# Attention output projection in a decoder trunk: two partial sums moved into the residual, twelve products beside each step, and one norm's squares summed on VectorE

## The chip, the cores and the metric

The kernel runs on one core of one Trainium2 chip. A core has a matrix engine (TensorE, PE in the profile; its weight loads are PEld), VectorE (DVE), ScalarE (ACT), GpSimd (POOL) and SyncE (SP), which here issues the loads from memory. Each engine works through its own instructions in a fixed order and waits on semaphores where it needs another engine's result. Matrix products are accumulated in PSUM, of which the kernel uses all eight banks, each 128 partitions by 512 floats. The metric is the device time of one execution in microseconds (us), lower is better. Differences of about 0.2% (2.3 us) are as much as such a measurement can tell from no change.

## The reference

A trunk of two layers over 512 positions of width 1024. Layer 0 mixes tokens with a gated MLP, then a gated feed-forward part with a causal convolution, then a gated embedding. Layer 1 uses sliding-window attention with 16 query heads over 4 shared key/value heads; its output projection is added to the residual, and the same kind of feed-forward part follows. The part that matters here:

```python
def rmsnorm(x, g):
    xf = x.astype(jnp.float32)
    y = xf * lax.rsqrt(jnp.mean(xf * xf, axis=-1, keepdims=True) + EPS)
    return (y * g.astype(jnp.float32)).astype(x.dtype)

def mixer_b(xn, w_q, sinks, w_o, kblk, vblk):        # layer 1
    ...
    probs = e / (jnp.sum(e, axis=-1, keepdims=True) + jnp.exp(sink - m))
    out = jnp.einsum('bnkgij,bnjkd->bnikgd', probs.astype(vblk.dtype), vblk)
    return out.reshape(B, S, N_Q_HEADS * HEAD_DIM) @ w_o

# in the layer loop
h = h + mixer_b(xn, b_w_q[b], b_sinks[b], b_w_o[b], kblk, vblk)
h = h + conv_ffn(rmsnorm(h, norm_ffn[i]), f_w_up[i], f_conv_w[i], f_conv_b[i], f_w_down[i])
```

## The kernel before

**Layout.** Activations lie feature-major: the residual is eight tiles `h[0]` to `h[7]`, each 128 features by 512 positions. Every matrix product is done in a split form to keep float32 accuracy: both operands are cut into a high and a low part, and `mm3` (lines 184 to 192) issues three matmuls of 128x128 by 128x512 for each block of 128 rows of the contraction: high by high, high by low, low by high. In this text a *product* is one such matmul; a whole row block of 1024 features needs 8 x 3 = 24 products.

**Weights.** Weight pieces come from memory on SP's queue (`load`, line 136) into raw buffers, and each unit of 1024 columns is cut by ScalarE (`wh`, line 163) and VectorE (`wl`, line 164). There are four `wh` and four `wl` buffers. A piece of the output projection is 2048 columns, that is two units: unit one serves contraction blocks 0 to 3, unit two serves blocks 4 to 7, for two row blocks `m`. `chunk` asks for a piece, and `more` (line 741) asks for one unit ahead of its use.

**The attention stage.** Sixteen steps `i`, one for each of 4 head groups `g` and 4 blocks of 128 positions `n`, with `n` fastest. `scores(i)` makes the score products (`sc`, lines 793, 794), masks and takes minima on VectorE (lines 796, 800) and exponentials on ScalarE (805); `weights(i)` normalizes (813, 815); `turn(i)` transposes on the matrix engine (`tr`, 830) and cuts the result (`pts`, `p`, lines 261, 262; for `n` > 0 GpSimd masks a second copy, 838); `mix(i)` multiplies with the values (`pv`, 852; four products, two where `n` is 0) and `finish(i)` leaves two 128x128 pieces of the attention output in `o2[2g]` and `o2[2g+1]` (872, 875). So `o2[0:2]` belongs to group 0, `o2[2:4]` to group 1, `o2[4:6]` to group 2 (steps 8 to 11), `o2[6:8]` to group 3 (steps 12 to 15). The loop:

```python
for i in range(last + 2):            # last = 16, LATE = 14
    if i < last:
        with tc.high_priority():
            scores(i)
    if LATE <= i < last + 1:
        finish(i - 3)
    if i <= last:
        fill(i)
    if i >= 2:
        mix(i - 2)
    ...
        with tc.high_priority():
            turn(i - 1)
```

**Work beside the steps.** `fill(i)` issues what the table `beside` (line 745) lists for step `i`: other products that keep the matrix engine fed while a step's softmax runs on the other engines. Steps 0 to 9 carry the query projections of later groups, twelve products or more each. Steps 10 to 17 carry parts of the output projection: `merge(m, k0, k1)` (line 732) adds contraction blocks `k0` to `k1` of row block `m` into its PSUM bank `o{m}`, which it holds from its first block to its last. In the table of before, steps 10 to 12 have 12 products, step 13 has 9, step 14 has 15, step 15 has 12, and steps 16 and 17 have 18 each.

**After the steps** (lines 906 to 911) each row block gets its missing products, VectorE adds the bank to `h[m]` (line 910), and `nf.take(m)` (line 295) prepares the next norm: ScalarE scales and rounds (`nf10h`, 257), VectorE makes the low part (`nf10l`, 258), ScalarE squares (`nf1sq`, 287), and GpSimd adds the squares up (`nf1acc`, line 292), all but the last block's, which VectorE adds. The feed-forward part starts on `nf10h`, `nf10l`. Its first up-projection `up(0)` has two halves of 24 products; between them, in the matrix engine's order, stand the products of `norm.begin()` (`nf1ms`, 312), which need the complete sum of squares turned and reduced on VectorE (`nf1turn` 302, `nf1quarter` 304).

**Order.** A scheduler orders each engine's instructions ahead of time, by the program's order as priority, and takes a later instruction first where an earlier one is not ready by its own estimate. PSUM banks and weight buffers are given from a pool of free ones. Lines 190 to 192, 163, 164, 257, 258, 261, 262, 287 and 292 are helpers shared by all stages, so a row is told apart by its tile names.

Of the kernel before, what the change touches and what calls it, by code (L numbers as in the profile page):

```python
# [13 lines left out]
P = 128  # L14
D = 1024
S = 512
KD = D // P
# [31 lines left out]
def tile_yoco(ctx: ExitStack, tc: tile.TileContext, t, out: bass.AP, out_b: bass.AP):  # L49
    nc = tc.nc  # L50
# [10 lines left out]
    def psum(name):  # L61
        return mmp.tile([P, S], F32, tag="mm", name=name)
# [111 lines left out]
    def chunk(cols, kk, ahead=WBUFS):  # L174

        pump(state["next"] + ahead)
        parts = []
        while len(parts) < kk:
            wh, wl, n = take()
            parts += [(wh, wl, j * cols) for j in range(n // cols)]  # L180
        assert len(parts) == kk
        return parts

    def mm3(ps, parts, xs, c0, n=P, first=True, last=True):

        for k, ((wh, wl, off), (xh, xl)) in enumerate(zip(parts, xs)):
            a, b = off + c0, off + c0 + n
            st = first and k == 0
            en = last and k == len(parts) - 1
            nc.tensor.matmul(ps, wh[:, a:b], xh, start=st, stop=False)  # L190
            nc.tensor.matmul(ps, wh[:, a:b], xl, start=False, stop=False)  # L191
            nc.tensor.matmul(ps, wl[:, a:b], xh, start=False, stop=en)  # L192
# [19 lines left out]
    h = [hp.tile([P, S], F32, tag=f"h{k}", name=f"h{k}") for k in range(KD)]  # L212
# [141 lines left out]
    def gain(name, l=0):  # L354
        return lambda k: v(name, l * KD + k)
# [215 lines left out]
    for c in range(4):  # L571
# [4 lines left out]
        for j in range(2):  # L576
            m = 2 * c + j
# [18 lines left out]
    nf = Norm("nf0", [(xp, "x", gain("norm_ffn", 0))])  # L596
# [106 lines left out]
    box = {}  # L703
# [25 lines left out]
        if k1 == KD:  # L729
            qs[g] += queries(box["qp"], g, j)  # L730

    def merge(m, k0, k1):

        if m // 2 not in box:
            box[m // 2] = chunk(256, KD, ahead=2)
        if k0 == 0:
            box[f"o{m}"] = psum(f"o{m}")
        mm3(box[f"o{m}"], box[m // 2][k0:k1], o2[k0:k1], m % 2 * P, first=k0 == 0, last=k1 == KD)
        box[f"k{m}"] = k1

    def more():

# [12 lines left out]
        8: [(project, 3, 1, 0, 4)],  # L755
        9: [(project, 3, 1, 4, 8)],
        10: [(merge, 0, 0, 2), (merge, 1, 0, 2), (more,)],
        11: [(merge, 2, 0, 2), (merge, 3, 0, 2), (more,)],
        12: [(merge, 0, 2, 4), (merge, 1, 2, 4), (more,)],
        13: [(merge, 2, 2, 4), (merge, 3, 2, 3)],  # L760
        14: [(merge, 3, 3, 4), (merge, 0, 4, 6), (merge, 1, 4, 6)],
        15: [(merge, 2, 4, 6), (merge, 3, 4, 6)],
        16: [(merge, 4, 0, 6)],
        17: [(merge, 5, 0, 6)],
    }

    def fill(i):
# [3 lines left out]
    o2 = [[ap.tile([P, S], F32R, tag=f"a{x}{m}", name=f"o{x}{m}") for x in "hl"] for m in range(KD)]  # L771
# [105 lines left out]
    last = len(steps)  # L877
# [28 lines left out]
    nf = Norm("nf1", [(xp, "x", gain("norm_ffn", 1))])  # L906
    for c in range(4):
        for m in (2 * c, 2 * c + 1):
            merge(m, box.get(f"k{m}", 0), KD)
            nc.vector.tensor_add(h[m], h[m], box[f"o{m}"])  # L910
            nf.take(m)

    npl = Norm("np1", [(xp, "x", gain("norm_ple", 1))])
    pef, pet = ffn(1, nf, npl)
# [4 lines left out]
    first = [(a[:, half], b[:, half]) for a, b in xs]  # L919
# [215 lines left out]
```

## Time and profile before

| what | us |
|---|---|
| time, median of 3 runs | 1144.05 |
| lowest and highest of these runs | 1143.8, 1144.77 |
| the profiled execution's own time | 1145.29 |
| its span, first to last instruction | 1143.6 |
| matrix engine busy in the span | 1129.7 |
| VectorE busy | 750.5 |
| ScalarE busy | 521.3 |
| GpSimd busy | 124.5 |
| HBM traffic | 96 GB/s over the span |

The profile is of one execution. Its rows give start and duration in us from the span's start; the number in square brackets behind a row of the timeline is how long the engine stood idle before it, with the instruction that ended the wait. Matmuls are pipelined: a 128x512 product is shown with 0.39 us but follows the one before it after about 0.23 us, so starts are compared and durations of matmuls are not added. In tables by stretch the columns are the length, then busy time and number of instructions of PE, PEld, DVE, ACT and POOL, then the granted clock of the matrix engine (1.00 is full), the share of the DMA engines and their rate.

### The profile page before, as it was taken

The numbers are of one execution on the slowest core, as the hardware profiler recorded it, in microseconds if no ns is written. First come the engines' busy times: TensorE is split into PE (matmuls) and PEld (weight loads), VectorE is DVE, ScalarE is ACT, GpSimd is POOL, SyncE is SP. The second block draws the span as 40 slices with busy tenths as digits, with TensorE's granted clock in tenths as the row PEclk, the third lists the DMA queues.
The fourth block names the chain that finished last, engine by engine and source line by source line (L and its number), as shares of the span: only waits on it lengthen the run. The fifth ranks groups of instructions, "written<-read, shape, count | busy, mean of one in ns | idle before, by whom it ended". The sixth has DMA issues, their size and how long they took to land.

```text
span 1143.6 us, 13592 instructions
## 1 busy us (share of the span) xinstructions
PE 1129.7 (99%) x5266; PEld 942.5 (82%) x5266; DVE 750.5 (66%) x1142; ACT 521.3 (46%) x843; POOL 124.5 (11%) x191
## 2 busy tenths in 40 slices
PE   9999999999999999999999989999999999999997
PEld 7888888888888888888898877788888888888896
DVE  7366477762677367557988967777636763675675
ACT  6534344441343235445656865444313432355562
POOL 2000300000000000021124654000000000000222
PEclk9999999999999999999999999999999999999999
DMA  8322323323223322332224413223232233224302
GB/s 299 144 81 74 111 77 108 110 75 111 93 83 101 111 92 75 129 111 74 74 74 129 129 39 143 83 106 111 74 111 99 76 101 111 92 76 165 111 1 74
DMA packets 25775, 115.40 MB, mean 101 GB/s; under 512 B 2920, under 2 KB 8176, under 8 KB 16240
## 3 DMA queue, kind: packets, MB, share of 16 engines
q1 hardware_dynamic: 25152, 113.89, 29.4%
q8 instruction: 41, 0.67, 0.2%
q10 hardware_dynamic: 560, 0.66, 0.2%
q14 instruction: 22, 0.18, 0.1%
HBM read 108.24 MB, written 2.11 MB: 96 GB/s over the span
## 4 chain that ended last, share of the span: by engine, by line
PE 93%; DVE 4%; issue 1%; ACT 1%; DMA 0%; POOL 0%; SPq 0%; POOLq 0%; DVEq 0%
PE up L190 14%; PE up L191 14%; PE up L192 14%; PE d L190 8%; PE d L192 8%; PE d L191 8%; PE gate L190 2%; PE gate L191 2%; PE gate L192 2%; PE q L190 1%; PE q L192 1%; PE q L191 1%; PE u L191 1%; PE u L192 1%; PE u L190 1%
## 5 line engine op out<-in xcount | busy, mean ns | idle before, releaser
L163 ACT CAST wh<-wraw 128x1024 fp32r<-128x1024 f32 (+2 forms) x197 | 201.8, 1028 | 264.7 <-PE d L191 123.9
L164 DVE TENSOR_TENSOR wl<-wraw,wh 128x1024 fp32r<-128x1024 f32 (+1 forms) x198 | 239.2, 1209 | 126.4 <-ACT wh L163 126.1
L191 PE MATMUL up<-nf10l,wh 128*128 128x512 f32 x352 | 137.8, 391 | 0.4 <-DVE nf10l L258 0.4
L190 PE MATMUL up<-nf10h,wh 128*128 128x512 f32 x352 | 137.7, 391 | 0.0
L192 PE MATMUL up<-nf10h,wl 128*128 128x512 f32 x352 | 137.5, 391 | 0.0
L190 PE MATMUL up<-nf00h,wh 128*128 128x512 f32 x352 | 137.1, 390 | 0.0
L191 PE MATMUL up<-nf00l,wh 128*128 128x512 f32 x352 | 136.9, 389 | 0.0
L192 PE MATMUL up<-nf00h,wl 128*128 128x512 f32 x352 | 136.9, 389 | 0.0
L190 PE MATMUL d<-ah,wh 128*128 128x512 f32 x352 | 136.9, 389 | 0.0
L191 PE MATMUL d<-al,wh 128*128 128x512 f32 x352 | 136.9, 389 | 0.0
L192 PE MATMUL d<-ah,wl 128*128 128x512 f32 x352 | 136.9, 389 | 0.0
L389 ACT ACTIVATE c<-hs,vec 128x512 f32<-128x512 f32 x88 | 71.5, 814 | 72.1 <-DVE hs L385 71.3
L390 DVE SCALAR_TENSOR_TENSOR c<-hs,vec,c 128x511 f32<-128x511 f32 x88 | 65.8, 749 | 34.4 <-ACT c L389 34.4
L365 DVE TENSOR_TENSOR h<-h,d 128x512 f32<-128x512 f32 x56 | 38.4, 687 | 73.6 <-PE d L192 73.6
L191 PEld LDWEIGHTS up<-nf10l,wh 128*128 128x128 f32 x352 | 66.4, 189 | 14.4 <-DVE nf10l L258 0.8
L192 PEld LDWEIGHTS up<-nf10h,wl 128*128 128x128 f32 x352 | 66.5, 189 | 13.9
L190 PEld LDWEIGHTS up<-nf10h,wh 128*128 128x128 f32 x352 | 66.5, 189 | 13.9
L191 PEld LDWEIGHTS up<-nf00l,wh 128*128 128x128 f32 x352 | 66.1, 188 | 13.8
L191 PEld LDWEIGHTS d<-al,wh 128*128 128x128 f32 x352 | 66.1, 188 | 13.7
L192 PEld LDWEIGHTS d<-ah,wl 128*128 128x128 f32 x352 | 66.1, 188 | 13.7
L190 PEld LDWEIGHTS d<-ah,wh 128*128 128x128 f32 x352 | 66.1, 188 | 13.7
L192 PEld LDWEIGHTS up<-nf00h,wl 128*128 128x128 f32 x352 | 66.1, 188 | 13.6
(455 smaller groups left out, 2032.2 us busy)
## 6 DMA issues: line engine op xcount, KB each, us to landing
wraw<-in_w_up SPq DMA_DIRECT2D x44, 1024.0 KB, 4.8
wraw<-in_w_down SPq DMA_DIRECT2D x16, 896.0 KB, 4.6
wraw<-in_w_down SPq DMA_DIRECT2D x8, 1024.0 KB, 4.8
wraw<-in_w_gate SPq DMA_DIRECT2D x8, 1024.0 KB, 4.8
wraw<-in_w_u SPq DMA_DIRECT2D x4, 1024.0 KB, 5.7
wraw<-in_w_out SPq DMA_DIRECT2D x4, 1024.0 KB, 4.7
wraw<-in_w_q SPq DMA_DIRECT2D x4, 1024.0 KB, 4.9
wraw<-in_w_o SPq DMA_DIRECT2D x4, 1024.0 KB, 5.0
```

The source lines that it names most:

```text
L163: nc.scalar.copy(hi, src)
L164: nc.vector.tensor_sub(low, src, hi.bitcast(F32))
L190: nc.tensor.matmul(ps, wh[:, a:b], xh, start=st, stop=False)
L191: nc.tensor.matmul(ps, wh[:, a:b], xl, start=False, stop=False)
L192: nc.tensor.matmul(ps, wl[:, a:b], xh, start=False, stop=en)
L365: nc.vector.tensor_add(h[m], h[m], ps)
L389: nc.scalar.activation(c, hs, AF.Identity, bias=v("conv_b", l * 2 * NJ + col), scale=cw[2])
L390: nc.vector.scalar_tensor_tensor(c[:, 1:], hs[:, : S - 1], cw[1], c[:, 1:], op0=ALU.mult, op1=ALU.add)
```

## The change

Three things. `merge` gets an argument `leave`: it closes the sum after the blocks done so far, VectorE adds the bank to `h[m]`, and the bank is free; the next `merge` of that row block opens a new bank, whose sum is added to `h[m]` later. The table `beside` is rewritten from step 11 on: row blocks 0 and 1 leave after blocks 0 to 3, the steps 11 to 15 have twelve products each from `o2[0:4]`, step 16 has 24 from `o2[4:6]`, and step 17 has none. In the loop after the steps, `nf.take(m)` becomes `nf.split(m, 0)` and `nf.square(m, nc.vector)`: the squares are still made by ScalarE, but all seven additions of squares are VectorE's.

```diff
-    def merge(m, k0, k1):
+    def merge(m, k0, k1, leave=False):
         if m // 2 not in box:
             box[m // 2] = chunk(256, KD, ahead=2)
-        if k0 == 0:
-            box[f"o{m}"] = psum(f"o{m}")
-        mm3(box[f"o{m}"], box[m // 2][k0:k1], o2[k0:k1], m % 2 * P, first=k0 == 0, last=k1 == KD)
-        box[f"k{m}"] = k1
+        first = k0 == 0 or box.get(f"left{m}", False)
+        if first:
+            box[f"o{m}"] = psum(f"o{m}_{k0}")
+        mm3(box[f"o{m}"], box[m // 2][k0:k1], o2[k0:k1], m % 2 * P, first=first, last=leave or k1 == KD)
+        box[f"k{m}"], box[f"left{m}"] = k1, leave
+        if leave:
+            nc.vector.tensor_add(h[m], h[m], box[f"o{m}"])
...
         10: [(merge, 0, 0, 2), (merge, 1, 0, 2), (more,)],
-        11: [(merge, 2, 0, 2), (merge, 3, 0, 2), (more,)],
-        12: [(merge, 0, 2, 4), (merge, 1, 2, 4), (more,)],
-        13: [(merge, 2, 2, 4), (merge, 3, 2, 3)],
-        14: [(merge, 3, 3, 4), (merge, 0, 4, 6), (merge, 1, 4, 6)],
-        15: [(merge, 2, 4, 6), (merge, 3, 4, 6)],
-        16: [(merge, 4, 0, 6)],
-        17: [(merge, 5, 0, 6)],
+        11: [(merge, 2, 0, 2), (merge, 0, 2, 4, True), (more,)],
+        12: [(merge, 1, 2, 4, True), (merge, 2, 2, 4)],
+        13: [(merge, 3, 0, 4), (more,)],
+        14: [(merge, 4, 0, 4)],
+        15: [(merge, 5, 0, 4)],
+        16: [(merge, 2, 4, 6), (merge, 3, 4, 6), (merge, 0, 4, 6), (merge, 1, 4, 6)],
...
             merge(m, box.get(f"k{m}", 0), KD)
             nc.vector.tensor_add(h[m], h[m], box[f"o{m}"])
-            nf.take(m)
+            nf.split(m, 0)
+            nf.square(m, nc.vector)
```

`Norm.split` and `Norm.square` are the two halves of `take`; `square(m, eng)` runs the addition on `eng`:

```python
def square(self, k, eng=None):
    sq = tp.tile([P, S], F32, tag="sq", name=f"{self.name}sq{k}")
    nc.scalar.activation(sq, h[k], AF.Square)
    if self.acc is None:
        self.acc = sq
    else:
        acc = tp.tile([P, S], F32, tag="acc", name=f"{self.name}acc{k}")
        (eng or nc.gpsimd).tensor_add(acc, self.acc, sq)
        self.acc = acc

def take(self, k):
    self.split(k, 0)
    self.square(k, nc.vector if k == KD - 1 else None)
```

## The prediction

> **What bounds the kernel now.** First the page's busy times, then the table by stretch, to see where the matrix engine is not fed.
>
> ```profile
> PE 1129.7 (99%) x5266; PEld 942.5 (82%) x5266; DVE 750.5 (66%) x1142; ACT 521.3 (46%) x843; POOL 124.5 (11%) x191
> ```
>
> ```profile
> core 0: us, PE busy (x) PEld busy (x) DVE busy (x) ACT busy (x) POOL busy (x), PEclk, DMA share, GB/s
> 608.00:648.00 40.00, 40.00 (x225) 34.34 (x224) 36.56 (x107) 32.67 (x100) 21.41 (x37) 1.00 0.41 111
> 648.14:657.94 9.80, 9.80 (x55) 8.28 (x54) 8.94 (x32) 7.85 (x29) 6.00 (x12) 1.00 0.56 162
> 657.94:663.58 5.64, 5.34 (x30) 4.40 (x28) 4.54 (x15) 4.66 (x16) 4.16 (x7) 1.00 0.00 0
> 667.98:676.77 8.79, 5.98 (x26) 4.25 (x25) 7.57 (x26) 6.66 (x22) 4.86 (x8) 0.83 0.34 120
> 689.46:712.93 23.47, 23.47 (x104) 19.26 (x103) 18.50 (x21) 13.73 (x24) 10.97 (x10) 1.00 0.39 143
> 145.28:156.51 11.23, 11.23 (x53) 9.33 (x51) 8.20 (x16) 3.12 (x5) 1.02 (x1) 1.00 0.27 94
> 712.93:727.93 15.00, 13.29 (x52) 10.22 (x50) 10.10 (x17) 4.77 (x8) 2.32 (x2) 0.89 0.34 127
> ```
>
> The matrix engine sets the time nearly everywhere; a change can gain only where it is starved. Attention steps with twelve products beside them (608 to 648) leave it no gap. Steps 14 and 15 (667.98 to 676.77) do: 2.8 us idle, and a granted clock of 0.83. The second place is the first up-projection after the attention: the same work took 11.23 us in layer 0 (145.28) and 15.00 us here, **3.8 us** lost. The timeline of the matrix engine shows both:
>
> ```profile
> 648.14 0.39 PE L190 MATMUL o<-oh,wh 128*128 128x512 f32 x1
> 650.89 0.39 PE L852 MATMUL pv<-pts,vt 128*128 128x512 f32 x1
> 652.74 0.40 PE L190 MATMUL o<-oh,wh 128*128 128x512 f32 x1
> 657.94 0.40 PE L190 MATMUL o<-oh,wh 128*128 128x512 f32 x1
> 672.87 0.36 PE L793 MATMUL sc<-kh,q 128*128 128x256 f32 x1 [1.86 <-DVE p13l L262]
> 676.77 0.70 PE L190 MATMUL o<-oh,wh 128*128 128x512 f32 x1
> 686.89 0.60 PE L830 MATMUL tr<-ident,prs 128*128 128x128 f32 x4
> 712.93 0.39 PE L190 MATMUL up<-nf10h,wh 128*128 128x512 f32 x1
> 718.45 0.50 PE L191 MATMUL up<-nf10l,wh 128*128 128x512 f32 x1 [0.37 <-DVE nf10l L258]
> 720.52 0.39 PE L312 MATMUL nf1ms<-nf1quarter,alike 128*128 128x16 f32 x2 [1.33 <-DVE nf1quarter L304]
> ```
>
> At 672.87 score products waited for a PSUM bank that a transpose still held, with no product able to run: row blocks 0 to 3 held four banks, and the next products needed the head pieces of step 11. At 720.52 the engine waited for VectorE.
>
> **The attention stage, part by part.** Twelve products take 650.89 - 648.14 = 2.75 us (0.229 each). The rest of a step (scores, transposes, mix) takes 652.74 - 650.89 = 1.85 us with two mix products; by 657.94 - 652.74 = 5.20 a whole step with four takes about 5.1 us, one with two 4.6. Nothing before step 11 differs, and I keep 657.94 as the start of step 12's products. After the change steps 12, 13 and 14 are alike, since no product beside them needs a piece younger than step 7: 657.94 + 5.1 + 5.1 + 4.6 = 672.7 starts step 15's twelve. These take 2.75, mix and transpose 1.4, step 16's 24 products 5.5, mix and the last transpose 1.4: 683.8, against 686.89 + 0.60 = 687.5 before. I leave 0.2 for bank waits (0.30 idle in the stretch from 657.94): **3.5 us earlier**. Banks held are fewer than before in steps 12 to 14; at step 16 all six open row blocks hold one, where it was five. Price if that costs a wait like the largest here, 1.86; if none, 0. I take 0, because 24 products stand between opening them and the next mix.
>
> The two leaving additions are VectorE's, between step 12's masks and minima, which ScalarE's exponentials wait for. By line 910's rows below each is 0.68 us. In the stretch from 648.14 VectorE idles 0.86 us, in the next 1.1, and twelve products cover each step: 0. Without that cover 1.4 us. Moving `more` from step 12 to 13 adds no load and no instruction; the converted unit is first needed in step 16, about two steps later: 0. On SP the queue keeps its order; no DMA is added.
>
> **After the steps.** Before, 18 products of row block 5 stood between the last mix and the first product that needs its result. Now there are none in program order. The last transpose ended at 687.5 and the last piece was ready at 693.5:
>
> ```profile
> 693.01 0.49 DVE L875 TENSOR_TENSOR ol<-side,oh 128x128 fp32r<-128x128 f32 x2 [0.72 <-ACT oh L872]
> 695.45 0.69 DVE L910 TENSOR_TENSOR h<-h,o 128x512 f32<-128x512 f32 x1
> 719.78 0.69 DVE L304 TENSOR_REDUCE nf1quarter<-nf1turn 128x16 f32<-128x512 f32 x1
> 145.35 0.69 DVE L365 TENSOR_TENSOR h<-h,d 128x512 f32<-128x512 f32 x1 [0.64 <-PE d L192]
> 149.53 0.69 DVE L304 TENSOR_REDUCE nf0quarter<-nf0turn 128x16 f32<-128x512 f32 x1
> ```
>
> These 6.0 us stay. To fill them are the mixes and whatever the scheduler pulls forward: blocks 4 and 5 of row blocks 4 and 5 (12 products) and blocks 0 to 5 of 6 and 7, as a bank comes free. It took mixes ahead of waiting products before, so I expect it to. Either way VectorE's first residual addition (695.45) moves with the last piece, to 692.0.
>
> **VectorE's chain.** From there VectorE works almost without pause to 720.47, 25.0 us. What it does there, and the same forms undisturbed:
>
> ```profile
> L258 DVE SCALAR_TENSOR_TENSOR nf10l<-h,vec,nf10h 128x512 fp32r<-128x512 f32 x8 | 8.9, 1135 | 0.8 <-ACT nf10h L257 0.8
> L164 DVE TENSOR_TENSOR wl<-wraw,wh 128x1024 fp32r<-128x1024 f32 x6 | 8.7, 1455 | 1.4 <-ACT wh L163 1.4
> L292 POOL TENSOR_TENSOR nf1acc<-nf1acc,nf1sq 128x512 f32<-128x512 f32 x5 | 8.2, 1646 | 5.5 <-ACT nf1sq L287 5.4
> L257 ACT ACTIVATE nf10h<-h,vec 128x512 fp32r<-128x512 f32 x8 | 5.7, 718 | 8.4 <-DVE h L910 8.4
> L287 ACT ACTIVATE nf1sq<-h 128x512 f32<-128x512 f32 x8 | 5.0, 622 | 0.6 <-POOL nf1acc L292 0.5
> L910 DVE TENSOR_TENSOR h<-h,o 128x512 f32<-128x512 f32 x8 | 5.3, 680 | 0.8 <-PE o L192 0.7
> L258 DVE SCALAR_TENSOR_TENSOR np00l<-h,vec,np00h x8: 746/749/752, 484.6 to 518.5; 128x512 fp32r<-128x512 f32 x8
> L292 DVE TENSOR_TENSOR n0acc<-n0acc,n0sq x6: 684/688/694, 13.4 to 20.7; 128x512 f32<-128x512 f32 x6
> L164 DVE TENSOR_TENSOR wl<-wraw,wh 128x1024 fp32r<-128x1024 f32 (+1 forms) x198 | 239.2, 1209 | 126.4 <-ACT wh L163 126.1
> ```
>
> The low parts took 1135 ns here and 749 elsewhere, the weight cuts 1455 against 1209; the residual additions, with one operand in PSUM, kept 680. GpSimd's additions of squares, 1646 ns each, ran beside these, so I put the excess down to them: 8 x 0.386 + 6 x 0.246 = 4.6 us. The change removes that and gives VectorE six more additions of 0.688, 4.1 us: nearly a draw. The list after: 8 residual additions 5.4, 8 low parts 6.0, 7 additions of squares 4.8, 5 weight cuts 6.0 (one of the six came before 695.45), turn and reduction 1.4: 23.7. The same list of before: 5.3 + 8.9 + 7.5 + 0.7 + 1.4 = 23.8, for 25.0 measured, so 1.2 went in waits net of overlap. Between no such waits (23.7) and the same (24.9) I take the middle, **24.3**: the reduction ends at 692.0 + 24.3 = 716.3, which is **4.2 us earlier**, 3.5 by the earlier start and 0.7 by the chain.
>
> The matrix engine would be there first. After 683.8 it has a mix (0.9), 96 products (22.0) and the first half of the up-projection (5.5): 712.2 without any wait. So VectorE sets the end of this stage, and I keep all that followed the reduction before, the slow matmuls too.
>
> The sum against the profiled execution's own time: 1145.3 - 4.2 = 1141.1 (span 1143.6 - 4.2 = 1139.4). The median of the runs shown is 1.2 below that execution, so the forecast is 1144.05 - 4.2 = **1139.8**.
>
> [...]
>
> **The rivals.**
> (1) *VectorE keeps up.* The two weight cuts for the second up-projection are not needed before the reduction; put behind it, they take 2.4 from the list, and overlap of neighbours does the rest: VectorE must be done in 712.2 - 692.0 = 20.2. Then the first up-projection starts at 706.7 instead of 712.93 and loses nothing: 6.2 + 3.8 = 10.0, **1134.0**. For it: layer 0 lost nothing, with 149.53 + 0.69 - 145.35 = 4.9 us from the last addition to the reduction. Against: before, both cuts ran ahead of it.
> (2) *Nothing fills the 6.0 us.* The 96 products start at 690.0: 690.0 + 22.0 + 5.5 = 717.5, later than VectorE; 3.0 gained, **1141.0**. For it: the removed 18 products stood right there. Against: the products are independent, and the scheduler reorders.
> (3) *Slower: VectorE in lock step with ScalarE.* Each addition of squares now stands in VectorE's own queue and must wait for ScalarE's rounding and square of that row block (0.72 + 0.62); what is queued behind it, the next residual addition and the next low part, which the up-projection waits for, stops with it. At full price, 8 x 1.34 = 10.7 on top of 23.7, the reduction ends at 726.4, 5.9 later: **1150.0**. It decides from 720.5 - 692.0 - 23.7 = 4.8 us of such waits, 0.6 a row block. For it: GpSimd waited 5.4 us for squares. Against: VectorE waited only 0.8 for the rounded parts, having other blocks' work to take.
> (4) *The clock stays full.* The 3.8 lost in the up-projection less its two waits, 1.7, is 2.1 of slow matmuls; without them **1137.7**. Against: both stretches with waits under 2 us show 0.83 and 0.89.
> (5) *It does not do what it says:* the step stall only moves, for instance because the bank wait of 1.86 recurs in step 15 or 16 with its slow matmuls. Then 0.7 of the chain is left: **1143.3**.
>
> **How the numbers follow.** Forecast 0.42, rival (1) 0.22, (2) 0.10, (3) 0.15, (4) 0.04, (5) 0.07. 0.2% is 2.3 us, about what a measurement of this kernel can tell from no change. Faster by more than that: forecast, (1), (2) and (4), less a little for their edges, 0.76; the same: (5) and those edges, 0.09; slower 0.15. The range runs from below (1), 1133.2, to 1146.5, halfway to (3); the forecast's own, with chain lengths of 23.7 to 24.9 and up to 1.9 for a bank wait, is 1139.2 to 1142.3.
>
> **What would show it.** Right: products of steps 12 to 15 follow each other without idle time and at clock 1.00; step 16's products end near 682.5; no addition of squares on GpSimd in this norm, and low parts near 749 ns; the norm's product still waits for VectorE, near 716.4. The attention step is wrong if a score or mix product waits over 1 us after step 12; the cover is wrong if the matrix engine idles some 4 us after the last mix; the chain is wrong if VectorE idles over 4.8 us before the reduction, or if low parts stay above 1 us without GpSimd. The forecast as a whole fails if the first up-projection begins later than 712.9.

## The result

The changed kernel takes 1137.83 us (median of 4 runs, 1137.49 to 1138.2) where the kernel before takes 1143.92 beside it (1143.78 to 1144.77): the ratio is 0.9945, with a 95% interval of 0.9928 to 0.9963. It is faster by 6.1 us. The profiled execution spans 1136.2 us, 7.4 less than before; its own time is 1137.98. The profiled execution of before (1145.29) was 1.4 us above the median given here, so the spans differ by more than the medians.

The page of the changed kernel, busy times:

```profile
PE 1125.2 (99%) x5266; PEld 939.9 (83%) x5266; DVE 751.4 (66%) x1150; ACT 521.3 (46%) x843; POOL 114.2 (10%) x185
```

The stage by stretches, with the same columns as before the change (length, then PE, PEld, DVE, ACT and POOL busy, clock, DMA share and rate):

```profile
...
652.77:659.49 6.72, 5.54 (x30) 4.17 (x29) 5.78 (x20) 4.74 (x19) 4.01 (x8) 1.00 0.63 195
659.49:677.00 17.51, 17.51 (x95) 14.94 (x94) 15.37 (x50) 14.33 (x48) 11.44 (x20) 1.00 0.18 61
677.00:683.81 6.81, 6.81 (x33) 5.64 (x32) 4.67 (x9) 3.92 (x12) 3.93 (x7) 1.00 0.01 4
683.81:690.25 6.44, 5.46 (x25) 3.80 (x23) 1.54 (x4) 3.33 (x9) 3.56 (x6) 1.00 0.36 114
690.25:709.45 19.20, 19.20 (x85) 15.84 (x86) 16.99 (x25) 12.27 (x20) 0.00 (x0) 1.00 0.39 139
709.45:720.57 11.12, 11.12 (x51) 9.16 (x50) 8.61 (x17) 3.35 (x5) 1.01 (x1) 1.00 0.44 168
```

From step 12 (659.49) to the last mixes the matrix engine has no idle time and the clock stays at 1.00; the stretch that before held 2.8 us of waits at a clock of 0.83 is gone. Two waits are left, 1.2 us in step 11 (652.77 to 659.49) and 1.0 us behind the last mix (683.81 to 690.25). The up-projection takes 11.12 us, as in layer 0, where it took 15.00. The matrix engine's timeline shows where these stretches begin and end (behind the changed lines, line numbers are 3 higher than before):

```profile
656.00 0.50 PE L191 MATMUL o<-ol,wh 128*128 128x512 f32 x1 [1.00 <-POOL ol L878]
...
659.49 0.40 PE L190 MATMUL o<-oh,wh 128*128 128x512 f32 x1
...
684.05 0.60 PE L833 MATMUL tr<-ident,prs 128*128 128x128 f32 x4
...
690.25 0.73 PE L190 MATMUL o<-oh,wh 128*128 128x512 f32 x2 [0.98 <-ACT oh L875]
...
709.45 0.39 PE L190 MATMUL up<-nf10h,wh 128*128 128x512 f32 x1
...
714.89 0.30 PE L312 MATMUL nf1ms<-nf1quarter,alike 128*128 128x16 f32 x2
...
720.57 0.40 PE L348 MATMUL nf1sp<-nf1dh,ones 128*128 128x512 f32 x1
```

Step 12's products start at 659.49, not at 657.94: in step 11 a product waited for the low part that GpSimd was still making. From there all is earlier: the last transpose ends at 684.65 (687.5 before), the up-projection starts at 709.45 (712.93), and the norm's product at 714.89 follows without a wait. VectorE's timeline and its groups from 690 to 721:

```profile
690.24 0.49 DVE L878 TENSOR_TENSOR ol<-side,oh 128x128 fp32r<-128x128 f32 x2 [0.70 <-ACT oh L875]
692.18 0.69 DVE L913 TENSOR_TENSOR h<-h,o 128x512 f32<-128x512 f32 x1 [1.45 <-PE o L192]
...
714.05 0.69 DVE L304 TENSOR_REDUCE nf1quarter<-nf1turn 128x16 f32<-128x512 f32 x1
```

```profile
L164 DVE TENSOR_TENSOR wl<-wraw,wh 128x1024 fp32r<-128x1024 f32 x6 | 7.2, 1222 | 0.6 <-ACT wh L163 0.6
...
L258 DVE SCALAR_TENSOR_TENSOR nf10l<-h,vec,nf10h 128x512 fp32r<-128x512 f32 x8 | 6.0, 746 | 0.0
...
L913 DVE TENSOR_TENSOR h<-h,o 128x512 f32<-128x512 f32 x8 | 5.5, 684 | 1.9 <-PE o L192 1.9
...
L292 DVE TENSOR_TENSOR nf1acc<-nf1acc,nf1sq 128x512 f32<-128x512 f32 x6 | 4.1, 686 | 0.0
```

Between the first residual addition and the end of the reduction VectorE takes 714.74 - 692.18 = 22.6 us, with six more additions in it; before it took 25.0. Low parts take 746 ns, where they took 1135. The 7.4 us of span divide so: the last piece of attention output is ready 2.8 us earlier (690.73 against 693.5), the way from there to the end of the reduction is 3.0 us shorter, and the matmuls from the norm's product (720.52 before, 714.89 now) to the next helper product (727.93, 720.57) take 5.7 us where they took 7.4, since none is slow. Slow matmuls stand in the profile of before in two stretches of 3.41 us at a granted clock of 0.50, one in steps 14 and 15 and one behind the norm's product (their rows are in the last section); the changed kernel has none in this stage. In the second stretch products start 0.43 us apart (721.90 to 724.46), where they otherwise start 0.23 apart. By an estimate from these rows a stretch costs up to half its length, 1.7 us, and the two up to 3.4 of the 7.4 us of span.

### The profile page after: what moved, and what is told of

Same layout as the page of the kernel before. It is cut to its first block, busy times and chain, and to the rows that moved or that the text cites. A ratio compares the mean times of both kernels' runs of the same rounds, so it can differ in the third digit from the quotient of the medians.

```text
span 1136.2 us, 13591 instructions
## 1 busy us (share of the span) xinstructions
PE 1125.2 (99%) x5266; PEld 939.9 (83%) x5266; DVE 751.4 (66%) x1150; ACT 521.3 (46%) x843; POOL 114.2 (10%) x185
## 4 chain that ended last, share of the span: by engine, by line
PE 92%; DVE 3%; issue 1%; ACT 1%; DMA 1%; POOL 1%; SPq 0%; POOLq 0%; DVEq 0%; ACTq 0%
PE up L192 14%; PE up L190 14%; PE up L191 14%; PE d L192 8%; PE d L191 8%; PE d L190 8%; PE gate L190 2%; PE gate L192 2%; PE gate L191 2%; PE u L191 1%; PE u L192 1%; PE u L190 1%; PE o L191 1%; PE o L190 1%; PE o L192 1%
## 5 line engine op out<-in xcount | busy, mean ns | idle before, releaser
L261 ACT CAST ah<-a 128x512 fp32r<-128x512 f32 x44 | 27.4, 622 | 109.5 <-DVE a L395 109.4
L190 PEld LDWEIGHTS up<-nf00h,wh 128*128 128x128 f32 x352 | 66.1, 188 | 13.6
```

The lines of the kernel that those rows point to most:

```text
L261: ins = nc.scalar.copy(hi, src)
```

## The experiments

Each time stands beside runs of the kernel before on the same chip, and the ratios compare chips; smaller differences are read between kernels that ran together.

### The table alone, and the squares alone

```diff
 # e1_table_only, from the changed kernel
-            nf.split(m, 0)
-            nf.square(m, nc.vector)
+            nf.take(m)
 # e2_squares_only, from the kernel before
-            nf.take(m)
+            nf.split(m, 0)
+            nf.square(m, nc.vector)
```

> The new table with the leaving sums, but the squares of the norm after the attention added by GpSimd as before (take in place of split and square). Theory (two separate gains: the table moves the last piece of attention output from 693.5 to 690.7, and the squares shorten VectorE's stretch from first residual addition to reduction): that stretch is again about 25 us with low parts near 1.1 us, the reduction ends near 692.2 + 25.0 = 717.2, the norm's product waits some 2.5 us for it behind an up-projection that starts near 709.5, and the matmuls behind it run slowly; the time is 1143.9 - 2.8 = 1141.1. Rival (the matrix engine alone sets the end, GpSimd's additions cost nothing): 1137.8, as with the whole change.

Measured 1141.91 us beside 1144.1, ratio 0.9978 (0.9967 to 0.9988), 0.8 us above the theory's 1141.1. VectorE's and GpSimd's groups of this kernel from 690 to 721, and the matrix engine's timeline:

```profile
L258 DVE SCALAR_TENSOR_TENSOR nf10l<-h,vec,nf10h 128x512 fp32r<-128x512 f32 x8 | 10.0, 1263 | 0.8 <-ACT nf10h L257 0.8
L292 POOL TENSOR_TENSOR nf1acc<-nf1acc,nf1sq 128x512 f32<-128x512 f32 x5 | 7.5, 1501 | 7.2 <-ACT nf1sq L287 7.0
```

```profile
709.00 0.39 PE L190 MATMUL up<-nf10h,wh 128*128 128x512 f32 x1
...
717.03 0.56 PE L312 MATMUL nf1ms<-nf1quarter,alike 128*128 128x16 f32 x2 [1.34 <-DVE nf1quarter L304]
...
724.43 0.40 PE L348 MATMUL nf1sp<-nf1dh,ones 128*128 128x512 f32 x1
```

The up-projection starts as early as in the changed kernel, but low parts take 1263 ns beside GpSimd's additions of 1501, the norm's product comes 2.1 us later (717.03) after a wait of 1.34, and slow matmuls follow (7.4 us to 724.43). The theory holds: the table moves the stage forward, and the end waits for VectorE.

> The table and merge of before, only the squares after the attention are added by VectorE. Theory (GpSimd's reads slowed VectorE, and without them its stretch takes 22.6 us as in the changed kernel): first residual addition at 695.5 as before, reduction done at 718.1, before the first up-projection half ends at 718.4, so the norm's product does not wait and the 3.8 us lost in the first up-projection come back: 1140.1. Rival (what the prediction took: six additions of 0.688 against 4.6 us of contention, a draw of 0.7): reduction at 719.8, slow matmuls stay, 1143.2. Second rival (VectorE is the bound and gets 4.1 us more): 1148.

Measured 1141.43 beside 1144.1, ratio 0.9970 (0.9958 to 0.9983). VectorE's and the matrix engine's timelines of this kernel:

```profile
695.57 0.69 DVE L910 TENSOR_TENSOR h<-h,o 128x512 f32<-128x512 f32 x1
...
717.39 0.69 DVE L304 TENSOR_REDUCE nf1quarter<-nf1turn 128x16 f32<-128x512 f32 x1
```

```profile
713.05 0.39 PE L190 MATMUL up<-nf10h,wh 128*128 128x512 f32 x1
...
718.50 0.29 PE L312 MATMUL nf1ms<-nf1quarter,alike 128*128 128x16 f32 x2
...
724.19 0.40 PE L348 MATMUL nf1sp<-nf1dh,ones 128*128 128x512 f32 x1
```

The first residual addition is where it was before (695.57), the reduction ends at 718.08, and the norm's product, wanted at 718.50, does not wait: the up-projection takes 11.1 us again. The span is 3.8 shorter, as the theory had it, though the median gained only 2.7. The stall of steps 14 and 15 stayed (1.85 us in front of 672.86), and with it its slow matmuls (products 0.43 us apart from 676.75 to 678.03). Neither the draw that the prediction took nor the overloaded VectorE came. The two halves nearly add up: 0.22% and 0.30% against 0.55% for the whole.

### GpSimd beside VectorE

The cost by itself: the changed kernel, with additions on GpSimd that nobody waits for.

```diff
             nf.square(m, nc.vector)
+            if m:
+                nc.gpsimd.tensor_add(side[:, 2 * S : 3 * S], h[m], h[m - 1])
```

> The changed kernel, and after each row block but the first GpSimd also adds two residual tiles into a scratch tile that nobody reads: seven additions of the old size, with no work of VectorE's behind them. Theory (GpSimd's reads slow those VectorE instructions that read two operands from SBUF): low parts go from 746 ns to 1.1 to 1.3 us each on the mean and weight cuts above 1.3, residual additions stay at 0.68; VectorE's stretch grows by about 4 us, the reduction ends near 718.5, the norm's product waits for it and slow matmuls follow: 1142 to 1144. Rival (the excess of before came from the order of the work, not from GpSimd): 1137.8 to 1138.3, low parts below 0.8 us.

Measured 1144.83 beside 1143.66, ratio 1.0012 (1.0003 to 1.0021): the whole gain is lost. Its groups from 690 to 725:

```profile
L917 POOL TENSOR_TENSOR side<-h,h 128x512 f32<-128x512 f32 x7 | 13.0, 1863 | 15.6 <-DVE h L913 11.2 <-ACT nf1sq L287 4.3
...
L258 DVE SCALAR_TENSOR_TENSOR nf10l<-h,vec,nf10h 128x512 fp32r<-128x512 f32 x8 | 9.4, 1172 | 0.0
L292 DVE TENSOR_TENSOR nf1acc<-nf1acc,nf1sq 128x512 f32<-128x512 f32 x6 | 6.3, 1044 | 0.0
...
L913 DVE TENSOR_TENSOR h<-h,o 128x512 f32<-128x512 f32 x8 | 5.4, 678 | 1.9 <-PE o L192 1.9
```

The scratch additions took 1863 ns each. Low parts rose from 746 to 1172 ns and the additions of squares from 686 to 1044; residual additions, with one operand in PSUM, stayed at 678. The weight cuts kept 1211, where the theory had them above 1.3 us. Rows of VectorE's, GpSimd's and the matrix engine's timelines show how:

```profile
704.07 0.74 DVE L258 SCALAR_TENSOR_TENSOR nf10l<-h,vec,nf10h 128x512 fp32r<-128x512 f32 x1
...
705.93 1.21 DVE L164 TENSOR_TENSOR wl<-wraw,wh 128x1024 fp32r<-128x1024 f32 x1
706.15 2.14 POOL L917 TENSOR_TENSOR side<-h,h 128x512 f32<-128x512 f32 x1 [2.56 <-DVE h L913]
707.07 1.77 DVE L258 SCALAR_TENSOR_TENSOR nf10l<-h,vec,nf10h 128x512 fp32r<-128x512 f32 x1
707.20 0.50 PE L192 MATMUL o<-oh,wl 128*128 128x512 f32 x1 [3.35 <-DVE wl L164]
```

The excess is not spread over the instructions. One that meets no addition keeps its length (0.74 us at 704.07), and so does one that had begun before the addition, as the weight cut at 705.93 and two more cuts like it. The addition then ends 1.15 us after the end of that instruction (708.29 against 707.14), and the low part behind takes 1.77 us, until 0.55 us after the addition. These two distances recur within 0.01 us for the last five of the seven additions. So in these rows the two engines take turns, each waiting for the other's end, and a meeting cost VectorE 1.0 to 1.1 us. The three weight cuts that met an addition had begun first and were spared. Six instructions of VectorE, three low parts and three additions of squares, take 1.77 or 1.78 us.

So GpSimd's additions do lengthen these VectorE instructions with two operands in SBUF (low parts from 746 to 1172 ns on the mean, additions of squares from 686 to 1044), and that is what the change's third part removes. That it is the reading of operands which collides, as the theory says, no run here separates. The size is above the expected: VectorE's stretch takes 28.9 us, 6.3 more and not 4, since the additions of squares grew too, and a product waited 3.35 us for a weight cut that was late behind the other work. The norm's product waited too, 1.34 us, but no slow matmuls followed in the profiled execution (clock 1.00 from 712 to 727).

### Is the freed bank needed

```diff
 def merge(m, k0, k1, leave=False):
+    leave = False
```

> The whole change, but no sum leaves PSUM: row blocks 0 and 1 keep their banks, and the two extra additions are gone. Six banks are then held by step 15 where the changed kernel holds four. Theory (the order of the products, not the banks, removed the stall): no score or mix product waits over 0.5 us, time 1137.8, or up to 1.4 less by the two additions. Rival (the freed banks matter): scores or transposes wait for a bank in steps 14 and 15 by 1 to 2 us each and the matmuls behind run slowly, 1140 to 1143.

Measured 1139.85 beside 1144.1, ratio 0.9958 (0.9943 to 0.9972). In the matrix engine's timeline of this kernel, the first product of step 10 and the one new wait behind step 12; in VectorE's, the first residual addition:

```profile
648.53 0.39 PE L190 MATMUL o<-oh,wh 128*128 128x512 f32 x1
...
671.34 0.47 PE L190 MATMUL o<-oh,wh 128*128 128x512 f32 x1 [1.21 <-DVE pts L262]
```

```profile
694.23 0.69 DVE L914 TENSOR_TENSOR h<-h,o 128x512 f32<-128x512 f32 x1 [1.45 <-PE o L192]
```

Scores and transposes did not wait; what waited, in step 14, was the first product of row block 4, which opens a fifth bank; the row names VectorE's cut of a transpose as what released it, after 1.21 us. The changed kernel has no such wait. By the ratios the time lies 1.1 to 1.5 us above the changed kernel's (0.9945 and 0.9948 of before in its two studies), though the intervals overlap. From the first product of step 10 to the first residual addition it takes 45.7 us here, 47.3 in the kernel before (648.14 to 695.45) and 44.0 in the changed kernel (648.17 to 692.18). So the order of the products brings 1.6 of the attention stage's 3.3 us, and the two sums that leave PSUM the other 1.7, of which this wait is 1.2. The theory holds in so far as no score or mix product waits, but not for the time; the rival was right that banks matter, but not on whom the wait falls, and no slow matmuls followed (clock 1.00 from 662 to 690).

### The wait in step 11

```diff
-        11: [(merge, 2, 0, 2), (merge, 0, 2, 4, True), (more,)],
-        12: [(merge, 1, 2, 4, True), (merge, 2, 2, 4)],
-        13: [(merge, 3, 0, 4), (more,)],
+        11: [(merge, 2, 0, 2), (merge, 3, 0, 2), (more,)],
+        12: [(merge, 0, 2, 4, True), (merge, 1, 2, 4, True)],
+        13: [(merge, 2, 2, 4), (merge, 3, 2, 4), (more,)],
```

> The changed kernel with steps 11 to 13 rearranged: step 11 has blocks 0 to 1 of row blocks 2 and 3, step 12 blocks 2 to 3 of 0 and 1, both leaving, step 13 blocks 2 to 3 of 2 and 3. Theory (in the changed kernel step 11's twelve products took 657.25 - 652.77 = 4.5 us in place of 2.75 because blocks 2 and 3 need the piece of step 7 that GpSimd ends at 656): these 1.7 us come back whole, everything behind moves, time 1136.1. Rival (VectorE's or ScalarE's own pace in steps 11 to 13 takes the place of the wait, or the four banks held at step 12 cost the 0.3 us of before): 1136.5 to 1137.8.

Measured 1137.12 beside 1144.1, ratio 0.9934 (0.9919 to 0.9949). Steps 10 to 15 by stretches:

```profile
648.14:662.00 13.86, 13.86 (x78) 11.73 (x78) 12.28 (x45) 11.43 (x41) 8.97 (x17) 1.00 0.39 115
662.00:677.00 15.00, 15.00 (x82) 12.59 (x81) 14.01 (x43) 11.66 (x38) 9.11 (x15) 1.00 0.21 72
```

No idle time is left there. The profile ended 1.2 us earlier than the changed kernel's, the length of the two waits, not the 1.7 that the step was longer. To tell so small a difference, both ran again on one chip:

> The changed kernel itself, on the same chip as the three beside it, so that differences under 0.2% can be told: 0.9945 of before within its interval, about 1137.8.

> The rearranged steps 11 to 13 again, beside the changed kernel. Its profile had no idle time in steps 11 to 16 and ended 1.2 us earlier, the length of the wait that went. Theory (the wait is the whole difference): 1.2 us below the changed kernel. Rival (it moved to where the time does not depend on it): within 0.3 us of it.

1138.32 and 1137.24 (ratios 0.9948 and 0.9938 to before): 1.1 us, as the theory had it. The ranges of the two, 1137.84 to 1138.49 and 1136.7 to 1137.47, do not meet.

### The wait behind the last mix

```diff
 # e5_cover_last_mix, from the changed kernel; e6_old_heads_and_cover, with step 11 to 13 rearranged too
-        16: [(merge, 2, 4, 6), (merge, 3, 4, 6), (merge, 0, 4, 6), (merge, 1, 4, 6)],
+        16: [(merge, 2, 4, 6), (merge, 3, 4, 6)],
+        17: [(merge, 0, 4, 6), (merge, 1, 4, 6)],
```

> The changed kernel with the twelve products of row blocks 0 and 1 (blocks 4 and 5) moved from step 16 to step 17, behind the last mix. Theory (VectorE sets the end here: the reduction ended 0.15 us before the norm's product wanted it, and VectorE starts when the last piece of attention output is ready): the 0.98 us idle behind the last mix goes, the last piece moves little, the first up-projection begins 1 us earlier and the norm's product then waits 0.8 to 1 us for the reduction: 1137.6 to 1138.6, no gain. Rival (the matrix engine sets the end): 1.0 less than the changed kernel, 1136.8. The last piece may also come up to 2.7 us earlier, because the last mix no longer stands behind these twelve products; then all moves by that and the time is 1135.5.

Measured 1138.17, on the chip where the changed kernel took 1138.32. VectorE's and the matrix engine's timelines:

```profile
690.02 0.69 DVE L914 TENSOR_TENSOR h<-h,o 128x512 f32<-128x512 f32 x1 [1.31 <-PE o L192]
...
714.33 0.69 DVE L304 TENSOR_REDUCE nf1quarter<-nf1turn 128x16 f32<-128x512 f32 x1
```

```profile
688.24 0.50 PE L190 MATMUL o<-oh,wh 128*128 128x512 f32 x1 [0.53 <-ACT oh L876]
...
710.00 0.39 PE L190 MATMUL up<-nf10h,wh 128*128 128x512 f32 x1
...
715.45 0.29 PE L312 MATMUL nf1ms<-nf1quarter,alike 128*128 128x16 f32 x2
```

The first residual addition came 2.6 us earlier than in the changed kernel's run beside it (690.02 against 692.65), and the end did not move: the up-projection starts at 710.00 (709.93 there), and the norm's product at 715.45 (715.37) follows without a wait. So no gain, as forecast, but not for the forecast reason: VectorE had 2.6 us more and did not set the end, the matrix engine did. VectorE spent the time in waits: its stretch took 25.0 us again, with 0.79 us for ScalarE's rounding, 0.64 for a weight and 0.64 for a product among them, though GpSimd adds nothing here. A wait of 0.53 us was left behind the last mix, though twelve products more stood there.

> Both rearrangements, steps 11 to 13 and the twelve products behind the last mix. Theory (gains add where both only move the last piece of attention output): the sum of the two differences, 1.2 from the first and what the second shows by itself.

Measured 1138.46, 1.2 us above the rearranged steps alone: a miss. With only twelve products beside step 16 the mix of step 14 waited 0.98 us for ScalarE's cut of the transpose, and 0.56 stayed behind the last mix. Together that is 0.5 us more than the one wait of 1.03 of the rearranged steps; the other 0.7 us is not explained. Two last arrangements therefore write down all that can fill the gap, and split it otherwise:

```diff
 # e8_six_behind_last_mix, with steps 11 to 13 rearranged
+        16: [(merge, 2, 4, 6), (merge, 3, 4, 6), (merge, 0, 4, 6)],
+        17: [(merge, 1, 4, 6), (merge, 4, 4, 6), (merge, 5, 4, 6)],
 # e9_twelve_behind_last_mix, the same
+        16: [(merge, 2, 4, 6), (merge, 3, 4, 6)],
+        17: [(merge, 4, 4, 6), (merge, 5, 4, 6), (merge, 0, 4, 6), (merge, 1, 4, 6)],
```

> Steps 11 to 13 rearranged as before, and of step 16's 24 products the six of row block 1 stand in step 17 behind the last mix, followed there by blocks 4 and 5 of row blocks 4 and 5 in writing. Theory (matrix engine sets the end; the 1.0 us idle behind the last mix is the only wait left in the stage, and 18 products ahead of the mix of step 14 still cover its inputs): idle there falls to 0.2 or less, up-projection begins 0.8 to 1.0 earlier, 1136.3. Rival (VectorE sets the end): no gain over the rearranged steps alone, 1137.2.

> As the one before, but all twelve products of row blocks 0 and 1 stand in step 17, behind the written-out twelve of row blocks 4 and 5; step 16 keeps 12. Theory: the mix of step 14 waits about 1 us for its inputs, as with both rearrangements (0.98 there), and nothing waits behind the last mix: 1137.2, no better than the rearranged steps alone.

> The rearranged steps 11 to 13 alone, for comparison on the same chip: 0.9938 of before within its interval, 1137.2.

Beside 1143.66 for the kernel before, the first took **1135.56** (ratio 0.9929, 0.9917 to 0.9942), the second 1136.87 (0.9940), and the rearranged steps alone 1136.80 (0.9940). All waits of the matrix engine in the first one, and the start of the up-projection in its timeline:

```profile
engine line waited for: us in total, times, longest us
PE idle L240 <- DVE minus_half L245: 1.1, 1, 1.1
PE v L203 <- DVE wl L164: 0.4, 1, 0.4
```

```profile
707.22 0.39 PE L190 MATMUL up<-nf10h,wh 128*128 128x512 f32 x1
```

It now waits for nothing but its start and, in layer 0, 0.4 us for a weight cut. That is 1.2 us better than the rearranged steps, about the length of the gap (0.99 there), and it beats the kernel before and the changed one. The second has the 0.98 us in front of the mix of step 14, as expected, and gains nothing.

## Why the prediction was right, and where not

The time lies inside the range of 1133.2 to 1146.5, and the sign and most of the parts were right. It lies below the forecast's own bounds, 1139.2 to 1142.3: the forecast of 1139.8 was 2.0 too high, 3.2 by the spans (1139.4 against 1136.2). Its picture of the end, which VectorE sets and slow matmuls follow, did not come. That it missed by no more is in part luck: waits that it did not count brought the matrix engine to the norm's product at 714.89 where it had reckoned 712.2, and so nearer to its own end of 716.3.

**The attention steps: right, but for step 11.** The prediction expected steps 12 to 15 without a gap and had them. It kept 657.94 as the start of step 12's products, on the ground that nothing before step 11 differs. Step 11 itself differs: its last products need the piece of step 7, which `finish` leaves only at the end of step 10. ScalarE's and GpSimd's last instructions for it stand among step 11's own, as this row of GpSimd's timeline in the changed kernel shows:

```profile
655.50 0.86 POOL L878 TENSOR_TENSOR ol<-side,oh 128x128 fp32r<-128x128 f32 x2
```

That cost 1.55 us at this place, and the rearranged steps brought back 1.1 of it. The last transpose came at 684.65 for 683.8, the last piece at 690.7 for 690.0, the first residual addition at 692.2 for 692.0.

**Banks: the price of 0 held** in the changed kernel. Without the leaving sums a product waits 1.21 us for a bank, and the stage is 1.7 us longer.

**The cover behind the last mix: as expected in kind.** The scheduler did put twelve products there, and 0.98 us stayed. The prediction had 4 us for no cover at all, and it did not add the remainder to its sum.

**VectorE's chain: the parts were right, the sum was not.** This is the step that failed. The list was costed at 23.7 us and comes to 23.8 from the rows of after (residual additions 5.5, low parts 6.0, squares 4.8, five cuts 6.1, turn and reduction 1.4). But it took 22.6: waits of 0.8 (0.45 and 0.3 us) against an overlap of neighbours of 2.0. The prediction added 0.6 for waits net of overlap, from the middle between none and those of before. Measured, that term is 1.2 the other way: against before, waits fell from 2.2 to 0.8 us and overlap grew from 1.0 to 2.0. So the chain gave 2.4 us where 0.7 was forecast. Where only the squares differ, the waits go with GpSimd's additions: 2.2 before and 0.7 with the squares alone, 2.0 with the table alone and 0.8 with both. They are not tied to them, since the kernel with twelve products behind the last mix has such waits again without any addition on GpSimd; what made them go is open. With that the forecast's picture of the end fell: VectorE ended 0.15 us ahead of the norm's product, not behind the matrix engine, and the 1.7 us of slow matmuls that the forecast kept did not come. Chain and start account for 1.6 of the 3.2 us, the slow matmuls for the rest.

**The rivals.** (1), VectorE keeps up, is what happened in the up-projection, with both weight cuts ahead of the reduction after all; its start of 706.7 came at 709.45, 2.5 of the 2.75 us by step 11 (1.55) and the wait behind the last mix (0.98). The forecast's time was still the nearer for the median. (2), no cover, was right by a quarter of its gap. (3), lock step with ScalarE, did not come: VectorE waited 0.3 us for ScalarE. (4) could not be told in the changed kernel, where nothing waits before these matmuls; that its 1137.7 is the number nearest to the result is chance. (5) would have shown as a wait over 1 us behind step 12: there is none before the last mix, though step 11's wait of 1.0 is of that kind.

The stage's last word is the matrix engine's, though VectorE was only 0.15 us ahead. That it is so was shown by the shift of VectorE's start by 2.6 us that moved nothing.

## What to carry to other kernels

An instruction moved to a busier engine was not charged by its own length alone here: VectorE took over six additions of 686 ns, and without GpSimd beside them its low parts fell from 1135 to 746 ns. With additions put back on GpSimd the price went by meetings, 1.0 to 1.1 us for each, and not by a share of all the work: a low part that met none kept its 0.74 us. Before a product is placed beside a step, the piece it needs should be looked up where it is finished on the last engine, not where the program issues it; here one step too early cost 1.1 us. The number of products in front of and behind a fixed latency had to be balanced: of the splits tried only 18 and 18 left no gap, 24 in front left one behind the last mix (0.98 us) and 12 one ahead of the mix of step 14 (0.98).

## What was not expected of the hardware

The slow matmuls did not follow from the size of the wait alone. They came in stretches of 3.41 us at a granted clock of 0.50. Leaving out the first and the last 8 us of each profile, there are two in the kernel before, one with the table alone, one with the squares alone (674.90 to 678.30), and none in the other kernels. The mean granted clock of the profiled execution is 0.996 in the kernel before, 0.997 in these two and 0.998 or 0.999 in the others. The two stretches of the kernel before, and the one of the table alone:

```profile
673.83:677.24 3.41, 3.02 (x9) 2.56 (x10) 2.05 (x9) 1.80 (x9) 1.76 (x4) 0.50 0.44 185
721.62:725.03 3.41, 3.41 (x10) 2.64 (x9) 1.55 (x5) 0.00 (x0) 1.02 (x1) 0.50 0.06 26
```

```profile
717.12:720.53 3.41, 3.41 (x9) 2.77 (x10) 1.69 (x8) 0.00 (x0) 1.02 (x1) 0.50 0.38 159
```

Three kernels had nearly the same two waits before the norm's product: 0.37 and 1.33 us in the kernel before, 0.54 and 1.34 with the table alone, 0.86 and 1.34 with GpSimd beside. The stretches there and after of the last:

```profile
718.00:721.00 3.00, 1.10 (x4) 0.30 (x2) 2.93 (x4) 0.00 (x0) 0.62 (x1) 1.00 0.80 279
721.00:724.00 3.00, 2.70 (x13) 2.27 (x14) 1.30 (x8) 0.00 (x0) 1.02 (x1) 1.00 0.17 71
```

Behind these waits the clock fell in the first two and stayed at 1.00 in the third, which had the longest idle time, and whose wait of 3.35 us at 707.20 brought no slow matmul either. Nor did single waits of 0.98 to 1.2 us in the other kernels. One program does not always do the same: of the eight executions of the table alone, on one chip, three with a mean granted clock of 0.999 span 1138.8 to 1139.2 us, four with 0.997, the profiled one among them, 1140.1 to 1140.7, and one with 0.995 1142.0. Half the clock for 3.41 us lowers the mean over 1140 us by 0.0015; by this estimate these fit none, one and two such stretches, at about 1.5 us each. The time of this kernel (1140.59 to 1143.74) therefore holds a part that differs from execution to execution.

What decides whether matmuls turn slow behind a wait no run here shows.
